# One layer of a hybrid backbone on one core: the kernel arranges every engine's instructions by its own account of durations

## The chip, the cores and the metric

The kernel runs on one core of a Trainium2 chip. The metric is device microseconds of one execution. The core has five engines that each run their own list of instructions in order: PE (matrix products), DVE and ACT (element-wise work), POOL and SP (which here mostly issue DMA transfers). "PEld" is PE's weight load, which runs beside its products. Instructions of different engines wait for each other through semaphores.

## The reference

One layer: two streams of 256 tokens (latent `x` and context `ctx`), width D = 2048, all in float32. The shift, scale and gate vectors come from two vectors `c` and `c_ctx` through one large matrix (adaLN), three mixers share one input projection, and a SwiGLU network follows.

```python
sh1_x, sc1_x, g1_x, sh2_x, sc2_x, g2_x = split(silu(c) @ w_mod + b_mod, 6)      # the same for c_ctx
hx = rmsnorm(x, norm1_g) * (1 + sc1_x) + sh1_x
hc = rmsnorm(ctx, norm1_g) * (1 + sc1_c) + sh1_c
zx, zc = hx @ w_in + b_in, hc @ w_in + b_in
s5_x = s5_mixer(zc[S5], zx[S5])            # diagonal state space, both directions, then a gated unit
ml_x = mlstm_mixer(zc[q, k, v, o, gates], zx[...])   # chunked matrix memory, both directions
cv_x = conv_module(zx[CONV])               # gated depthwise convolution and layer norm
x = x + g1_x * (concat(s5_x, cv_x, ml_x) @ w_out)
hx2 = rmsnorm(x, norm2_g) * (1 + sc2_x) + sh2_x
x = x + g2_x * ((silu(hx2 @ wg) * (hx2 @ wu)) @ w_ffn_out)
return rmsnorm(x, norm_f_g)
```

## The kernel before

**Weights.** All projection weights lie in `wst` as chunks of eight 128x128 tiles (512 KB). `raw_dma` fetches a chunk on SP's queue into `raw` (3 buffers). `split` turns it into two parts that sum to it: ACT casts `raw` to `whi` (L201, `acopy`), and DVE subtracts, `wlo = raw - whi` (L168, `tt`); 3 buffers each. The activations `hx` (latent) and `hc` (context) are held as two such parts too. `mm3` makes a product of three matmuls (whi with the high part, whi with the low part, wlo with the high part), `mm2` of two. All of these are issued by `mm` at L208 and use the whole 128x128 array at 256 or 512 columns.

**The first stage (28 to 146 us).** `main_kt` runs over 16 blocks `kt` of 128 input channels; each multiplies 7 weight tiles with the block's `hx` and `hc`, 42 matmuls, into seven accumulators (tags `ps_m`, `ps_qk`, `ps_b`). Before block `kt` can start, its `hx` and `hc` must exist, which need shift and scale of channel block `ft = kt`:

- `matvec_piece(ft, q)`, q = 0 to 3, multiplies a 512 KB piece of `w_mod` (tiles `wm`, `wmu`, `wmt`, seven buffers; DMA issued by POOL, the first ones by SP) with the vectors `cs`. It issues four matmuls at `tile_position` (0, 32 j), j = 0 to 3: each uses one strip of 32 columns of the array, with full float32 operands and 256 moving columns. These are called strips here; 16 of them make an `ft`. From `ft` = 1 on, all but the first are pinned to their place in the program (`keep_in_program_order`).
- `matvec_end(ft)`: ACT copies the result to `tmp`, PE transposes it twice (L403), DVE reduces to `as` and adds the biases.
- `make_h(ft)`: DVE normalises a block of `xr` and `cr` into `tmp`, ACT makes the high parts of `hx` and `hc` with `as` (L195), DVE the low parts.

The program writes `modulate(ft)` (the 16 strips) behind one tile of `main_kt` and `modulate2(ft)` (`matvec_end`, `make_h`) behind the next tile, some six tiles of work ahead of the block that needs them. `s5_params`, small DVE operations on 128x32 tiles (`wmt`, `s5c`, copies `LW`, `LC` at L552), is pumped in between.

**Later stages.** Up to 700 us the other tiles of the input projection and the output projection run on PE, with the S5, convolution and attention jobs as generators that `Sched` pumps between weight tiles by estimated engine time. Among their work: ACT copies `zT` to `U` (L201, x8 around 150 us) and `U` to `gT` (L201, x16 around 440 us); the gates (`rows`, transposed at L998 and L1000); and the remaining adaLN products, strips of 512 columns by groups of four. From 697 to 1448 us the SwiGLU network runs, and a final norm.

**What sets the order.** The program records instructions engine by engine; the Tile framework's scheduler then decides the order in which each engine executes them and which buffers they take, with its own estimates, except that an instruction given to `tc.keep_in_program_order` keeps its place.

Of the kernel before, what the change touches and what calls it, by code (L numbers as in the profile page):

```python
# [103 lines left out]
C_ID, C_MF, C_MR, C_K, C_SELG, NCST = 0, 128, 256, 384, 512, 640  # L104


class Sched:


    def __init__(self):  # L110
        self.pe = self.dve = self.act = 0.0
        self.jobs = []
# [34 lines left out]
            self.step(j)  # L147


@with_exitstack  # L150
def hybrid_layer_kernel(ctx: ExitStack, tc: tile.TileContext, xt, ctxt, wm1, wmr, wst, wg, bvrow, pvd, cstd, s5p, out):
    nc = tc.nc
    V, S, P, G = nc.vector, nc.scalar, nc.tensor, nc.gpsimd
# [2 lines left out]
    pre = prestack.enter_context(tc.tile_pool(name="pre", bufs=1))  # L156
    pp = ctx.enter_context(tc.tile_pool(name="pp", bufs=1, space=PSUM))
    sc = Sched()


    def n_of(ap):
        n = 1
        for s in ap.shape[1:]:
            n *= s
        return n

    def tt(o, a, b, op):
        V.tensor_tensor(out=o, in0=a, in1=b, op=op)  # L168
        sc.dve += 62 + 1.05 * n_of(o)
# [24 lines left out]
    def act(o, a, f, bias=0.0, scale=1.0, pin=False):  # L194
        i = S.activation(o, a, f, bias=bias, scale=scale)  # L195
        if pin:
            tc.keep_in_program_order(i)
        sc.act += 190 + 0.84 * n_of(o)

    def acopy(o, a):  # L200
# [3 lines left out]
    def mm(o, l, r, start, stop, native=False, tp=None, sgc=False, pin=False):  # L204
        kw = {}
        if tp is not None:
            kw["tile_position"] = tp
        i = P.matmul(o, lhsT=l, rhs=r, start=start, stop=stop, skip_group_check=sgc, **kw)  # L208
        if pin:
            tc.keep_in_program_order(i)  # L210
        n = n_of(o)
        sc.pe += (max(n * 4, 512) if native else max(n, 256)) / 2.36 / (1 if tp is None else 4)

# [12 lines left out]
    def tmp(n=512):  # L226
        return sb.tile([128, 512], F32, name="tmp", tag="tmp", bufs=4)[:, :n]
# [6 lines left out]
    cst = sb.tile([128, C_SELG], F32, name="cst")  # L234
# [22 lines left out]
    def raw_dma(c):  # L257
        raw[c] = sb.tile([128, CH * 128], F32, name="raw", tag="raw", bufs=3)
        i = nc.sync.dma_start(raw[c], wst[c])
        if phase1[0]:  # L260
            tc.keep_in_program_order(i)

    def split(c):
        his[c] = sb.tile([128, CH * 128], F32R, name="whi", tag="whi", bufs=3)
# [16 lines left out]
    def nxt(n=1):  # L281
        t = st["tile"]
        st["tile"] += n
        c, i = divmod(t, CH)
        if i == 0:
            if plan:
                plan_pump()
                fetch_to(c)
                split_to(min(c + SPL_LA, st["dma"] - 1))
            else:  # L290
                fetch_to(c + RAW_LA)
                split_to(c + SPL_LA)
        if i % PUMP_EVERY == 0:
            sc.pump()
        return his[c][:, i * 128:(i + n) * 128], los[c][:, i * 128:(i + n) * 128]

    def mm3(o, w, h, first, last, sgc=False):
        whi, wlo = w
        hhi, hlo = h
        mm(o, whi, hhi, first, False, sgc=sgc)  # L300
        mm(o, whi, hlo, False, False, sgc=sgc)
        mm(o, wlo, hhi, False, last, sgc=sgc)
# [5 lines left out]
        mm(o[:, 0:256], wlo, h[:, 0, :], False, last, sgc=True)  # L308

    def lnexp():  # L310
        tc.keep_in_program_order(S.preload_act_table_set("natural_log_exp_and_others"))

    def rsqrt(o, ps, n, scale, eps, epsv):

        y, t = tmp(n), tmp(n)
        act(y, ps, AF.Ln, bias=eps, scale=scale)
        act(y, y, AF.Exp, scale=-0.5)
        stt(t, y, -0.5 * scale, y, OP.mult, OP.mult)
        stt(t, ps, epsv / scale, t, OP.add, OP.mult)
        stt(o, t, 1.5, y, OP.add, OP.mult)  # L320
# [10 lines left out]
    def wm_dma(key, src, q=None):  # L331
        slot = (4 * key[0] + key[1]) % NWX if len(key) == 2 else 0
        if slot < NWM:
            wm[key] = sb.tile([128, 1024], F32, name="wm", tag="wm", bufs=NWM)
        else:
            wm[key] = wm_extra[slot - NWM]
        i = (q or nc.gpsimd).dma_start(wm[key], src)  # L337
        if q is not None:
            tc.keep_in_program_order(i)

    xr = pre.tile([128, KT, NT], F32, name="xr", tag="X")
    cr = sb.tile([128, KT, NT], F32, name="cr", tag="R1")
# [6 lines left out]
    def load_gates():  # L349
        wgr = tmp(256).rearrange("p (k n) -> p k n", k=KT)  # L350
        nc.sync.dma_start(wgr, wg)
        acopy(wgs[:, :, 0:16], wgr)
        tt(wgs[:, :, 16:32], wgr, wgs[:, :, 0:16], OP.subtract)
# [22 lines left out]
    cs = sb.tile([128, KT, 32], F32, name="cs")  # L376
    V.memset(cs, 0.0)
    act(cs[:, :, 0], pvc("c", 0, 16), AF.Silu)
    act(cs[:, :, 1], pvc("cc", 0, 16), AF.Silu)
    b1sc = sb.tile([128, 16], F32, name="b1sc")  # L380
# [193 lines left out]
    def main_kt(kt, hooks):  # L574
        n = 0
        for ct in range(4):
            w = nxt()
            mm3(s5b[ct][:, 256:512], w, (hx[:, kt, 0, :], hx[:, kt, 1, :]), kt == 0, kt == KT - 1, sgc=True)
            mm3(s5b[ct][:, 0:256], w, (hc[:, kt, 0, :], hc[:, kt, 1, :]), False, kt == KT - 1, sgc=True)
            hooks.get(ct, lambda: None)()  # L580
        for i in range(KHEAD):
            w = nxt()
            mm3(kb[i][:, 0:256], w, (hx[:, kt, 0, :], hx[:, kt, 1, :]), kt == 0, kt == KT - 1, sgc=True)
            mm3(kb[i][:, 256:512], w, (hc[:, kt, 0, :], hc[:, kt, 1, :]), False, kt == KT - 1, sgc=True)
            hooks.get(4 + i, lambda: None)()
# [4 lines left out]
    def modulate(ft):  # L590
        for q in range(4):
            matvec_piece(ft, q)
        plan_pump()

    def modulate2(ft):
        matvec_end(ft)
        make_h(ft)
# [7 lines left out]
    for kt in range(KT):  # L605
        hooks = {}
        for i in range(4 + KHEAD):
            t = (4 + KHEAD) * kt + i
            if t in hook_at:
                hooks[i] = lambda k=hook_at[t]: modulate(k)  # L610
            elif t - 1 in hook_at:
                hooks[i] = lambda k=hook_at[t - 1]: modulate2(k)
        main_kt(kt, hooks)
        if kt == 13:
            phase1[0] = False
            tc.keep_in_program_order(nc.sync.dma_start(cst[:, 128:], cstd[:, 128:C_SELG]))
            load_gates()
    sc.finish(pj)

# [155 lines left out]
    mj = sc.add(mod_job(), P_MOD)  # L775
# [233 lines left out]
    for ct in range(KHEAD, 8):  # L1009
        ps = mbank()  # L1010
        for kt in range(KT):
            w = nxt()
# [10 lines left out]
    for cb in range(2):  # L1023
# [3 lines left out]
        for kt in range(KT):  # L1027
            whi, wlo = nxt(4)
            for t in range(4):
                h = (hx if t < 2 else hc)[:, kt, :, 128 * (t % 2):128 * (t % 2) + 128]  # L1030
# [94 lines left out]
    q0 = st["tile"]  # L1125
# [41 lines left out]
    for ct in range(4):  # L1167
# [3 lines left out]
        sg, f = tmp(256), tmp(256)  # L1171
# [5 lines left out]
    for ct in range(KT):  # L1177
        ps = mbank()
        for i in range(8):
            src, j = (mx["c"], i) if i < 4 else (mixs, i - 4)  # L1180
# [105 lines left out]
    for kind, b in FSEQ:  # L1286
# [5 lines left out]
        last = b == NFF // FBLK - 1  # L1292
# [18 lines left out]
    i = 0  # L1311
    for n in (1, 1, 2, 2, 2, 2, 2, 2, 2):
        x = xres[:, i:i + n, :]
        tt(x, x, rs3[:, None, :].to_broadcast([128, n, NT]), OP.mult)
        nc.sync.dma_start(out[:, i:i + n, :], x)
        i += n

# [106 lines left out]
```

## Time and profile before

| | |
|---|---|
| median of 3 runs | 1461.98 us (1458.94 to 1462.68) |
| profiled execution | 1461.92 us |
| its span (first to last instruction) | 1460.2 us |
| PE busy | 1416.0 us, 97% of the span |
| PEld busy | 1242.3 us, 85% |
| DVE busy | 1058.8 us, 73% |
| ACT busy | 740.4 us, 51% |
| POOL busy | 107.3 us, 7% |
| HBM read | 311.55 MB |

A busy share is an average over stages with different limits. Rows of a timeline give start, duration, engine, line, operation, output<-inputs, count; the bracket at the end says how long the engine was idle before the row and which engine's instruction released it. Durations of single matmuls overlap (the next one enters the array while one drains), so the price of a group of matmuls is read from start to start. A full-float32 matmul that is no transpose leaves two records, so 16 strips read as x32.

### The profile page before, as it was taken

What the parts mean: (1) busy time and instruction counts of PE and PEld (TensorE: products, weight loads), DVE (VectorE), ACT (ScalarE), POOL (GpSimd) and SP (SyncE); (2) the same over time, 40 slices, a digit from 0 to 9 for tenths busy, and PEclk for the clock granted to TensorE, in tenths of its full rate; (3) what the DMA queues carried; (4) which work ended last, traced back from release to release, by engine and by line L of the source; (5) the groups of instructions that cost most, each with busy time, mean ns of one, the idle gap of its engine ahead of it and who ended that gap; (6) DMA issues with size and microseconds to landing.
All of it is one profiled execution on the core that took longest, in us unless ns stands there. A gap on an engine that the chain in (4) does not pass through costs nothing.

```text
span 1460.2 us, 25526 instructions
## 1 busy us (share of the span) xinstructions
PE 1416.0 (97%) x9856; PEld 1242.3 (85%) x9856; DVE 1058.8 (73%) x2104; ACT 740.4 (51%) x1279; POOL 107.3 (7%) x207
## 2 busy tenths in 40 slices
PE   6999899999999999999999999999999999999996
PEld 3888787887878999898998888888888888888885
DVE  7655699998988887888877778566555665556665
ACT  4334786654656555645555545433444334444353
POOL 1221111110001010011000010000000000000000
PEclk9999999999999999999999999999999999999998
DMA  9998464443436666689478787555555555555553
GB/s 365 359 359 300 156 234 142 164 165 117 143 120 226 219 238 236 243 310 343 145 234 278 277 299 240 187 189 186 189 188 187 187 188 188 188 188 188 188 177 112
DMA packets 87929, 315.31 MB, mean 216 GB/s; under 512 B 10096, under 2 KB 10880, under 8 KB 87808
## 3 DMA queue, kind: packets, MB, share of 16 engines
q1 hardware_dynamic: 60912, 216.67, 43.4%
q0 software_dynamic: 26896, 97.02, 18.8%
q8 instruction: 77, 1.26, 0.3%
q14 instruction: 44, 0.36, 0.1%
HBM read 311.55 MB, written 2.10 MB: 215 GB/s over the span
## 4 chain that ended last, share of the span: by engine, by line
PE 87%; DVE 5%; ACT 3%; DMA 2%; issue 1%; SPq 0%; DVEq 0%; ACTq 0%
PE ps_m L208 55%; PE ps_qk L208 20%; PE ps_b L208 12%; DMA raw<-in_wst_dram 1%; DVE tmp L168 1%; ACT whi L201 1%; DVE macc L179 1%; DVE wlo L168 1%; DMA tmp<-in_wg_dram 1%; ACT tmp L195 1%; PE ps_b L845 0%; ACT U L201 0%; PE ps_b L755 0%; DVE tmp L191 0%; DVE tmp L179 0%
## 5 line engine op out<-in xcount | busy, mean ns | idle before, releaser
L168 DVE TENSOR_TENSOR wlo<-raw,whi 128x1024 fp32r<-128x1024 f32 x386 | 471.3, 1222 | 268.0 <-ACT whi L201 264.4
L201 ACT CAST whi<-raw 128x1024 fp32r<-128x1024 f32 x386 | 403.8, 1047 | 478.8 <-PE ps_m L208 240.6
L208 PE MATMUL ps_m<-h,whi 128*128 128x512 f32 (+1 forms) x800 | 251.9, 369 | 3.5 <-ACT h L195 3.5
L208 PE MATMUL ps_m<-ffa,whi 128*128 128x512 f32 x704 | 248.8, 395 | 0.0
L208 PE MATMUL ps_qk<-h,whi 128*128 128x512 f32 (+1 forms) x688 | 233.2, 383 | 0.0
L208 PE MATMUL ps_m<-h,wlo 128*128 128x256 f32 x704 | 199.6, 284 | 0.0
L208 PE MATMUL ps_m<-ffa,wlo 128*128 128x256 f32 x704 | 198.9, 283 | 0.0
L208 PE MATMUL ps_m<-hx,whi 128*128 128x256 f32 x960 | 187.2, 291 | 5.5 <-ACT hx L195 3.6
L208 PE MATMUL ps_qk<-h,wlo 128*128 128x256 f32 x656 | 185.5, 283 | 0.0
L208 PEld LDWEIGHTS ps_m<-h,whi 128*128 128x128 f32 x800 | 144.9, 190 | 30.2 <-ACT h L195 4.0
L208 PEld LDWEIGHTS ps_m<-hx,whi 128*128 128x128 f32 x960 | 149.1, 190 | 24.7 <-issue 16.3
L208 PEld LDWEIGHTS ps_m<-ffa,whi 128*128 128x128 f32 x704 | 132.2, 188 | 32.2 <-issue 1.2
L208 PEld LDWEIGHTS ps_qk<-h,whi 128*128 128x128 f32 x688 | 127.2, 188 | 27.1
L179 DVE SCALAR_TENSOR_TENSOR macc<-wm,cs,macc 128x512 f32<-128x512 f32 x180 | 134.1, 745 | 6.2 <-ACT macc L195 3.8
L208 PE MATMUL ps_m<-hx,wlo 128*128 128x256 f32 x480 | 136.0, 284 | 0.0
L208 PEld LDWEIGHTS ps_m<-h,wlo 128*128 128x128 f32 x704 | 133.1, 189 | 0.0
L208 PEld LDWEIGHTS ps_m<-ffa,wlo 128*128 128x128 f32 x704 | 132.3, 188 | 0.1
L208 PEld LDWEIGHTS ps_qk<-h,wlo 128*128 128x128 f32 x656 | 123.3, 188 | 0.0
L337 POOL DMA_DIRECT2D wm<-in_wmr_dram x128 | 67.5, 528 | 607.7 <-DVE macc L179 431.3
L179 DVE SCALAR_TENSOR_TENSOR xres<-ps_m,mods,xres 128x256 f32<-128x256 f32 x160 | 76.9, 481 | 36.4 <-PE ps_m L208 34.4
L208 PEld LDWEIGHTS ps_m<-hx,wlo 128*128 128x128 f32 x480 | 91.2, 190 | 0.7 <-DVE wlo L168 0.7
L168 DVE TENSOR_TENSOR tmp<-tmp 128x256 f32<-128x256 f32 (+3 forms) x128 | 51.2, 410 | 6.1 <-ACT tmp L195 5.0
(268 smaller groups left out, 2135.7 us busy)
## 6 DMA issues: line engine op xcount, KB each, us to landing
raw<-in_wst_dram SPq DMA_DIRECT2D x386, 512.0 KB, 3.8
wm<-in_wmr_dram POOLq DMA_DIRECT2D x128, 512.0 KB, 5.3
wm<-in_wm_dram POOLq DMA_DIRECT2D x32, 512.0 KB, 7.0
wmu<-in_wm_dram POOLq DMA_DIRECT2D x16, 512.0 KB, 7.0
wmt<-in_wm_dram POOLq DMA_DIRECT2D x7, 512.0 KB, 5.8
wm<-in_wm_dram SPq DMA_DIRECT2D x5, 512.0 KB, 10.3
xr<-in_xt_dram SPq DMA_DIRECT2D x4, 512.0 KB, 6.0
cr<-in_ctxt_dram SPq DMA_DIRECT2D x4, 512.0 KB, 9.0
```

Of the source, the lines that this page charges most:

```text
L168: V.tensor_tensor(out=o, in0=a, in1=b, op=op)
L179: V.scalar_tensor_tensor(o, a, s, b, op0=op0, op1=op1)
L195: i = S.activation(o, a, f, bias=bias, scale=scale)
L201: S.copy(o, a)
L208: i = P.matmul(o, lhsT=l, rhs=r, start=start, stop=stop, skip_group_check=sgc, **kw)
L337: i = (q or nc.gpsimd).dma_start(wm[key], src)
```

## The change

The kernel no longer leaves the order to the framework. After all instructions are recorded, a new class `Arrange` reads them back, finds which ones depend on each other through the bytes they touch (`read_instructions`), gives each a duration (`account`), and places all of them by a list scheduler (`run`): at each step the engine that is free first takes, among the instructions whose inputs are ready by the account, the one that stands first in the program. Buffers of a tag go to the tiles in program order. `lay_down` then writes the order of each engine, and the turn of the buffers, as edges without semaphores, which the framework has to keep. `keep` replaces `keep_in_program_order`: a pinned instruction must follow the instruction that stands before it on its engine in the program. Arithmetic, tiles, DMAs and the number of instructions of each engine stay as they are. The tables `ranks` and `follows`, by which single instructions could be moved, are empty.

```diff
+class Arrange:
+    SEM, SAME, DMA, RATE = 45.0, 36.0, 1900.0, 345.0
...
+            if i.name in self.pins and e in last:
+                self.edge(last[e], k, 1)
...
+    def account(self, k, i, e, size):
...
+        if op == "DMACopy":
+            c = out[0][0] * out[0][3][0][1] * 4 / self.RATE
+        elif e == "PE":
+            cols = out[0][0]
+            f32r = "float32r" in str(size[0][2])
+            strip = i.tile_size[1] < 128
+            c = 6 + 0.4427 * cols if f32r else 109.0 if i.is_transpose else 2 * max(0.8438 * cols, 110.0)
+            self.mm[k] = (strip and not f32r, i.tile_position[1])
+        elif e == "DVE":
...
+            c = 150 + (2.0 if "is_tensor_tensor_scan=True" in text else 0.5 if op == "Memset" else 1.05) * n
+            c += 60 * scal
...
+        elif e == "ACT":
+            text = i.concise() if op == "Activation" else ""
+            c = 190 + 0.84 * n + 95 * scal - (40 if op == "TensorCopy" and psum else 0)
...
+    def run(self):
...
+        rank = [self.ranks.get(i.name, k) for k, i in enumerate(self.ins)]
...
+            if self.ins[k].opcode == "DMACopy":
+                clock[e] = s + (530.0 if e == "POOL" else 60.0)
+                pipe = max(s + self.DMA + (1200.0 if e == "POOL" else 0.0), pipe) + c
+                done = pipe
+            elif e == "PE":
+                strip, col = self.mm[k]
+                if strip:
+                    if strips.get("mode") != 1:
+                        s += 90
+                        strips["mode"] = 1
+                    s = max(s, strips.get(col, 0.0), strips.get("all", 0.0))
+                    strips[col] = s + c
...
+                else:
+                    s = max(s, strips.get("any", 0.0))
+                    strips["mode"] = 0
+                    clock[e] = strips["all"] = s + c
+                done = s + c + 170
...
+    def lay_down(self, engines):
+        for names in self.queue.values():
+            for s, t in zip(names, names[1:]):
...
+        for e in engines:
+            for a, b in zip(self.order[e], self.order[e][1:]):
+                self.tc.add_manual_dep(self.ins[b], self.ins[a].name, mybir.DependencyInfo(
+                    mybir.DependencyClass.NoSync, mybir.DependencyReason.DATA), reason="order")
...
+    def keep(i):
+
+        pins.add(i.ins.name)
...
-            tc.keep_in_program_order(i)
+            keep(i)
...
+    order = Arrange(tc, pins, ranks, follows)
+    order.run()
+    order.lay_down(("PE", "DVE", "ACT", "POOL", "SP"))
```

The lines of the helpers move by the new code: L208 becomes L498, L201 becomes L491, L195 becomes L485, L403 becomes L693. In the order lists below `wm`, `wmu`, `wmt` with `cs` are the strips of `matvec_piece`, the rows with `whi`, `wlo` the matmuls of `main_kt`, and `ps_b<-cst,tmp` the two transposes of `matvec_end`.

PE in the first stage, before: the strips for `ft` = 3 and, four matmul groups later, its transposes, early in block 2.

```order
71 L208 MATMUL ps_b<-wmu,cs 32x256 x4
72 L208 MATMUL ps_b<-wmt,cs 32x256 x4
73 L208 MATMUL ps_b<-wm,cs 32x256 x8
74 L208 MATMUL ps_m<-hx,whi 128x256 x2
75 L208 MATMUL ps_m<-hx,wlo 128x256
76 L208 MATMUL ps_m<-hc,whi 128x256 x2
77 L208 MATMUL ps_m<-hc,wlo 128x256
78 L403 MATMUL ps_b<-cst,tmp 128x128 x2
79 L208 MATMUL ps_m<-hx,whi 128x256 x2
80 L208 MATMUL ps_m<-hx,wlo 128x256
```

PE before, 24 rows later: the end of block 2, the strips for `ft` = 4, and the start of block 3.

```order
101 L208 MATMUL ps_b<-hc,whi 128x256 x2
102 L208 MATMUL ps_b<-hc,wlo 128x256
103 L208 MATMUL ps_b<-wm,cs 32x256 x8
104 L208 MATMUL ps_b<-wmu,cs 32x256 x8
105 L208 MATMUL ps_m<-hx,whi 128x256 x2
106 L208 MATMUL ps_m<-hx,wlo 128x256
107 L208 MATMUL ps_m<-hc,whi 128x256 x2
108 L208 MATMUL ps_m<-hc,wlo 128x256
109 L403 MATMUL ps_b<-cst,tmp 128x128 x2
```

PE with the change, at the end of block 2 and the start of block 3.

```order
102 L498 MATMUL ps_b<-hx,wlo 128x256
103 L498 MATMUL ps_b<-hc,whi 128x256 x2
104 L498 MATMUL ps_b<-wm,cs 32x256 x4
105 L498 MATMUL ps_b<-hc,wlo 128x256
106 L693 MATMUL ps_b<-cst,tmp 128x128 x2
107 L498 MATMUL ps_b<-wm,cs 32x256 x4
108 L498 MATMUL ps_m<-hx,whi 128x256
109 L498 MATMUL ps_b<-wm,cs 32x256 x4
110 L498 MATMUL ps_m<-hx,whi 128x256
111 L498 MATMUL ps_m<-hx,wlo 128x256
112 L498 MATMUL ps_m<-hc,whi 128x256 x2
113 L498 MATMUL ps_m<-hc,wlo 128x256
```

Two things moved. The 16 strips of an `ft`, which stood in one run behind the last tile of a block, now stand in pieces between matmuls of `main_kt`. And the transposes for `ft` = 3 (row 78 before, row 106 with the change), which stood almost a whole block ahead of block 3, now stand right before it, with four strips between them and the first matmul that reads what `make_h(3)` writes. In the whole order lists, the strips of 256 columns of `matvec_piece` stand in 18 runs before (14 of them of 16 strips) and in 48 with the change: 36 of 4, 9 of 8, 2 of 12 and 1 of 16. The work between the transposes of an `ft` and the first matmul that needs them is, before, 36 matmuls of `main_kt` and 16 strips for `ft` = 2 to 14. With the change it is 4 strips for `ft` = 1 and 3; 7 matmuls and 8 strips for `ft` = 2; 6 matmuls and 4 strips for `ft` = 4; 10 to 35 matmuls and up to 16 strips for the others.

ACT at the end of the first stage, before (`zT`, `kT` read the accumulators of the stage; `U` is a rearranged copy of `zT`).

```order
80 L201 CAST whi<-raw 128x1024
81 L201 COPY Wb<-tmp 64x16x16 x2
82 L195 ACTIVATE zT<-ps_m,pv 128x512
83 L195 ACTIVATE tmp<-cst,s5c 128x128
84 L195 ACTIVATE zT<-ps_m,pv 128x512 x2
85 L201 COPY Mb<-tmp 64x20x16
86 L195 ACTIVATE zT<-ps_qk,pv 128x512
87 L195 ACTIVATE kT<-ps_qk,bks 128x512
88 L201 COPY U<-zT 32x4x128
89 L195 ACTIVATE kT<-ps_b,bks 128x512 x2
90 L201 COPY U<-zT 32x4x128 x7
91 L201 CAST whi<-raw 128x1024 x2
```

ACT with the change, at the same place.

```order
75 L491 CAST whi<-raw 128x1024
76 L491 COPY bb<-bb 128x2x16
77 L485 ACTIVATE bb<-bb 128x2x16
78 L485 ACTIVATE zT<-ps_m,pv 128x512 x3
79 L491 COPY Wb<-tmp 64x16x16
80 L491 CAST wgs<-tmp 128x16x16
81 L485 ACTIVATE zT<-ps_qk,pv 128x512
82 L485 ACTIVATE kT<-ps_qk,bks 128x512
83 L485 ACTIVATE kT<-ps_b,bks 128x512 x2
84 L491 COPY U<-zT 32x4x128 x8
85 L491 CAST whi<-raw 128x1024 x3
```

The eight copies to `U` still stand ahead of the casts of the next weight chunks; ahead of them one `Wb` copy, an `Mb` copy and the `tmp` operation are gone to later places, and the cast `wgs` has come in, which stood 74th before. Around the sixteen copies to `gT` the order of ACT is, with one weight cast fewer or more beside them, the same as before, and on DVE the copies and operations on `gT` and `gs` still stand ahead of the `wlo` operations of the next chunks. From 750 us on PE's order is the same row by row, and DVE's and ACT's move by a place or two. SP's and POOL's orders are the same but for one or two places (the gate weights' DMA on SP, `bc` on POOL).

## Rows read from the trace of the kernel before

**Rows 1.** Windows: us, busy time of PE, PEld, DVE, ACT, POOL, clock, DMA share, GB/s

```profile
50.00:130.00 80.00, 80.00 (x840) 68.30 (x839) 42.28 (x111) 26.19 (x43) 21.90 (x42) 1.00 0.93 345
750.00:1448.00 698.00, 697.32 (x3983) 608.91 (x3983) 451.00 (x595) 323.45 (x471) 13.72 (x26) 1.00 0.61 204
```

**Rows 2.** PE's waits, 28 to 750 us: awaited, us in total, times, longest

```profile
PE ps_b L208 <- ACT whi L201: 4.1, 1, 4.1
PE ps_m L208 <- ACT hx L195: 3.6, 1, 3.6
PE ps_m L208 <- ACT whi L201: 1.7, 1, 1.7
PE ps_b L998 <- DVE rows L168: 1.4, 1, 1.4
PE ps_b L403 <- ACT tmp L201: 0.9, 1, 0.9
```

**Rows 3.** POOL's waits over the whole span, same columns

```profile
POOL wm L337 <- PE ps_b L208: 166.8, 24, 19.9
```

**Rows 4.** Timeline of PE, 67 to 70 us: last tile of a block, strips, next block

```profile
67.74 0.40 PE L208 MATMUL ps_b<-hc,whi 128*128 128x256 f32 x2
67.98 0.28 PE L208 MATMUL ps_b<-hc,wlo 128*128 128x256 f32 x1
68.19 0.64 PE L208 MATMUL ps_b<-wm,cs 128*32 128x256 f32 x8
68.65 1.05 PE L208 MATMUL ps_b<-wmu,cs 128*32 128x256 f32 x16
69.51 0.61 PE L208 MATMUL ps_b<-wmt,cs 128*32 128x256 f32 x8
70.05 0.50 PE L208 MATMUL ps_m<-hx,whi 128*128 128x256 f32 x2
```

**Rows 5.** Timeline of PE, 654 us: one run of four strips

```profile
654.64 0.28 PE L208 MATMUL ps_m<-mixm,wlo 128*128 128x256 f32 x1
654.85 0.64 PE L208 MATMUL ps_qk<-tmp,kc 128*32 128x256 f32 x8
655.42 0.51 PE L208 MATMUL ps_m<-mixm,whi 128*128 128x256 f32 x2
```

**Rows 6.** Timeline, 128 to 132 us: from transposes to `hx` of one `ft`

```profile
128.95 0.38 PE L403 MATMUL ps_b<-cst,tmp 128*128 128x128 f32 x2
...
130.10 0.60 ACT L195 ACTIVATE hx<-tmp,as 128x256 fp32r<-128x256 f32 x1 [1.40 <-DVE as L175]
...
130.61 0.59 ACT L195 ACTIVATE hc<-tmp,as 128x256 fp32r<-128x256 f32 x1
...
130.76 0.42 DVE L168 TENSOR_TENSOR hx<-tmp,hx 128x256 fp32r<-128x256 f32 x1
```

**Rows 7.** Timeline of DVE, 25 us: small copies in the start

```profile
25.56 0.40 DVE L552 COPY LC<-wmt 128x16 f32<-128x16 f32 x4
```

**Rows 8.** Timeline of ACT, 148 us: copies to `U`

```profile
148.98 7.81 ACT L201 COPY U<-zT 32x512 f32<-32x512 f32 x7
```

**Rows 9.** Windows behind or around three of those waits, columns as in rows 1

```profile
157.90:164.40 6.50, 6.48 (x22) 4.60 (x23) 4.00 (x4) 5.95 (x12) 0.00 (x0) 0.50 0.56 174
242.50:247.00 4.50, 3.59 (x28) 3.36 (x29) 4.34 (x9) 3.07 (x6) 0.00 (x0) 1.00 0.59 208
451.20:454.60 3.40, 3.40 (x14) 2.73 (x14) 3.40 (x4) 0.00 (x0) 0.08 (x1) 0.50 0.66 181
```

**Rows 10.** Timeline of PE, 306 to 310 us: a 512-column run, broken in two

```profile
307.03 1.04 PE L208 MATMUL ps_b<-wm,cs 128*32 128x512 f32 x2
308.01 1.10 PE L208 MATMUL ps_b<-tmp,Mb 128*128 128x64 f32 x8
...
309.71 1.06 PE L208 MATMUL ps_b<-wm,cs 128*32 128x512 f32 x6
```

**Rows 11.** Timeline of ACT, 439 us: copies to `gT`

```profile
439.37 6.88 ACT L201 COPY gT<-U 32x128 f32<-32x128 f32 x16
```

More of the change, by code (lines that the diff above doesn't have):

```diff
@@ L158, in hybrid_layer_kernel @@
     sc = Sched()
+    pins, ranks, follows = set(), {}, []
+    def keep(i):
+        pins.add(i.ins.name)
     def n_of(ap):
@@ L209, in mm @@
         if pin:
-            tc.keep_in_program_order(i)
+            keep(i)
         n = n_of(o)
@@ L260, in raw_dma @@
         if phase1[0]:
-            tc.keep_in_program_order(i)
+            keep(i)
     def split(c):
@@ L310, in lnexp @@
     def lnexp():
-        tc.keep_in_program_order(S.preload_act_table_set("natural_log_exp_and_others"))
+        keep(S.preload_act_table_set("natural_log_exp_and_others"))
     def rsqrt(o, ps, n, scale, eps, epsv):
@@ L338, in wm_dma @@
         if q is not None:
-            tc.keep_in_program_order(i)
+            keep(i)
     xr = pre.tile([128, KT, NT], F32, name="xr", tag="X")
@@ L615, in hybrid_layer_kernel @@
             phase1[0] = False
-            tc.keep_in_program_order(nc.sync.dma_start(cst[:, 128:], cstd[:, 128:C_SELG]))
+            keep(nc.sync.dma_start(cst[:, 128:], cstd[:, 128:C_SELG]))
             load_gates()
```

221 lines of the change are left out of this document (added).

## The prediction

> **What bounds the kernel now.** I read the windows first, then PE's waits, then the timelines of the places that the new order touches. From 750 us on PE is busy for 697.32 of 698 us, and between 50 and 130 us for 80.00 of 80, both at the full granted clock of 2.4 GHz [rows 1]. So in these two stretches any time that PE loses or saves is time of the kernel. The second thing to see is what PE waits for between 28 and 750 us [rows 2]. No row of that view names a DMA; the waits are for casts of weights on ACT (4.1 and 1.7 us), for the first `hx` (3.6), for the gates' `rows` (1.4) and for one `tmp` copy (0.9). The transfers of the adaLN pieces in turn wait for PE: POOL's queue stood 166.8 us for a buffer that PE had still to read [rows 3]. So the first stage goes at PE's pace, and what the order of PE costs there is paid in full.
>
> About 0.3% (4.4 us) is what a measurement of this kernel can tell from no change.
>
> **The change, part by part.** Nothing is computed more or less. The order lists show which places moved. From 750 us on PE's order is unchanged and PE never waits, so I count that stretch at nothing: DVE is busy 451.00 of its 698 us and ACT 323.45 [rows 1], which covers moves of a place or two on either. If that cover were gone, a late `wlo` would stop PE for at most the shift, about one operation.
>
> *Broken runs of strips, +6.8 us.* A run of strips has a price of its own beside its work. In one run of 16, the last whole-array matmul starts at 67.98 and the next one at 70.05, so 2.07 us; two whole-array matmuls take 0.24 from start to start (67.74 to 67.98), one 0.12, so the run costs 1.95 [rows 4]. A run of four: 654.64 to 655.42 is 0.78, less 0.12 is 0.66 [rows 5]. Twelve more strips cost 1.29, so four cost 0.43, and 0.23 of each run is the change of the array from whole to strips and back. The lists hold 48 such runs instead of 18. Thirty more at 0.227 (the rows before rounding) are 6.8 us, all in a stretch where PE has no free time. The kernel's own account charges 0.09 for a change, by which it would be 2.7; that is the lower bound, the measured rows decide for 6.8. A few of the new pieces stand before 35 us, where PE is still slow, so up to 8 is possible.
>
> *Transposes close to their use, +3.0 us.* From the transposes at 128.95 to the end of the high part of `hx` (130.10 + 0.60) is 1.75 us; the low part is done at 131.18, 2.23 behind the transposes [rows 6]. Before, 36 matmuls and 16 strips lie between (36 x 0.12 + 1.95 = 6.3 us), so nobody waits. With the change four strips (0.66) lie between for `ft` = 1 and 3: a wait of 1.1 us each; the second matmul comes behind another four strips, which cover the low part. For `ft` = 4 there are 6 matmuls and 4 strips, 0.72 + 0.66 = 1.38: 0.4 for the high part, and 0.3 more for the low one. For `ft` = 2, 0.84 + 1.09 in one run of eight or two of four: at most 0.1. The other eleven have 2.3 us or more. Together 3.0. At best none of it is new, where another wait comes first; at worst 4, where DVE is late with the reduction, since a `wlo` stands just ahead of it for `ft` = 4.
>
> Whether such a wait also costs clock is read from its neighbours. After the 1.7 us wait the granted clock was 0.50 (1.2 GHz) from 451.2 to 454.6; after the 4.1 us wait, from 157.9 to 164.4; around the 1.4 us wait it stayed 1.00 [rows 2, 9]. The new waits of 1.1 lie nearest to the 1.4, so I take no drop. The Trainium skill, page "TensorE: Matmul & The Clock Gate", section on HAM oscillation, describes a kernel in which waits for data put PE back to its lower clock tile after tile, each next tile starting cold. If that held for `ft` = 1, 3 and 4, the stretches behind them would run at half speed for a while, which is the third rival below.
>
> *The start, -0.4.* DVE's small copies `LC` and `LW` of `s5_params`, which stood between the operations that lead to the first `hx`, go behind them; PE waits for that `hx` [rows 2]. One row of them takes 0.40 [rows 7]. Other small operations come in their place, so the gain is between 0 and 1.
>
> *The cast of the gate weights, -0.9.* PE's last transposes wait 0.9 for a `tmp` copy [rows 2], which stood behind the cast `wgs` on ACT, and that cast waits for its DMA. The cast now comes some places later, when the data has long arrived. Between 0 and 0.9.
>
> *Broken runs made whole, -2.0.* Two runs of four strips with 512 columns stood as 1 + 3. Strips of one run work side by side, so the single one cost as much as a whole run: 307.03 to 308.01, 0.98 [rows 10]. Both are whole now. Between 0 and 2.0.
>
> *The gates' transposes, -1.2.* PE's transposes of `rows` stand some ten matmuls later, about 1.2 us, in front of a wait of 1.4 [rows 2]. At the same time DVE does other work ahead of the next `rows`. Between +1 and -1.4.
>
> *The copies to `U`, -0.5.* Seven of eight take 7.81 us on ACT [rows 8], and the cast that PE waits 4.1 us for is behind them. The order keeps that. Ahead of them `Wb`, `Mb` and a `tmp` operation have gone, and `wgs` has come. I take half a microsecond; the half clock stays. Between +1 and -2. The same for the sixteen copies to `gT`, 6.88 us [rows 11], in front of the 1.7 us wait: they keep their place, and I take 0, between +3 and -3.4.
>
> The sum is 6.8 + 3.0 - 0.4 - 0.9 - 2.0 - 1.2 - 0.5 = +4.8. The profiled execution took 1461.92 us (span 1460.2 and 1.7 around it), 0.06 under the median of the runs; so 1466.7 us. What the change gains lies in waits that are small, because the two long waits are kept by ACT operations that the account prices too low: it gives a copy to `U` 190 + 0.84 x 512 = 620 ns, where the row shows 7.81 / 7 = 1.12 us.
>
> **The rivals.**
>
> *A: the transfers set the pace of the first stage (faster).* If the DMA, not PE, decided when a block can go on, more runs of strips would fill time that PE spends waiting anyway, as the kernel's account believes (it reckons 345 GB/s). Then the 6.8 and the 3.0 vanish and -5.0 is left: 1456.9. For it: a DMA share of 0.93 at 345 GB/s [rows 1]. Against it: PE idles for nothing there, and POOL waits for PE [rows 1, 3]. It decides if PE in the present order would fall behind the transfers by less than the 9.8 us that the new order adds. Chance 0.17.
>
> *B: the long waits shrink enough (no change).* The wait of 4.1 us and the half clock behind it cost 4.1 + 6.5 / 2 = 7.3; those at 450 us 1.7 + 3.4 / 2 = 3.4 [rows 2, 9]. If the run of copies to `U` starts 2.7 us earlier, the wait falls to the 1.4 that did no harm, and 2.7 + 3.2 = 5.9 come back, 5.4 more than counted: 1461.3. With the other place too, 1457.9. For it: three ACT operations have gone from ahead of the copies. Against it: all eight copies still are there, and each takes over a microsecond. Chance 0.18.
>
> *C: the new waits take the clock down (slower by more).* If the waits before blocks 1, 3 and 4 are followed by 1.2 GHz as the 1.7 us wait was, each costs another 1.7 (half of 3.4) to 3.2 [rows 9]. Three times 2.2 is 6.5: 1473.2. It decides between waits of 1.4 and 1.7 us; mine are 1.1. Chance 0.13.
>
> **How the numbers follow.** The forecast has 0.52, A 0.17, B 0.18, C 0.13. The forecast's own spread, a few microseconds, lies on both sides of +4.4: 0.29 above, 0.21 between, 0.02 below -4.4. A gives 0.12 faster and 0.05 no change, B 0.06 and 0.12, C all slower. So faster 0.20, same 0.38, slower 0.42. The range runs from A's 1456 to C's 1474, which leaves out the cases where several bounds meet on one side; the forecast alone lies between 1461 and 1471.
>
> **What would show it.** In the profile after, a block of the first stage lasts 0.5 us longer (two more runs), and the stretch from the first `hx` to the last tile of block 15 some 9 us. PE's waits name ACT `hx` or DVE `hx` again, three to four times for about 1 us, all before 70 us. The waits for `whi` at 158 and 450 us stand there nearly unchanged with the half clock behind them, the wait for `tmp` before the last transposes is gone, and from 750 us on everything has the same length. I am wrong if the first stage is not longer (A), if the half clock near 158 us is missing (B), or if new stretches of 1.2 GHz appear in the first 70 us (C).

## The result and the profile after

| | before | after |
|---|---|---|
| median | 1461.23 us (4 runs, 1458.94 to 1462.68) | 1469.47 us (4 runs, 1467.0 to 1470.08) |
| ratio | | 1.0055, 95% interval 1.0036 to 1.0073 |
| profiled execution, its span | 1461.92, 1460.2 us | 1470.08, 1468.3 us |

The change makes the kernel 0.55% slower, 8.2 us. The forecast was 1466.7 us, 4.8 slower. The windows of the profile after answer to [rows 1]: between 50 and 130 us PE is no longer busy all the time, and from 750 us on it still is.

```profile
50.00:130.00 80.00, 78.81 (x735) 59.45 (x735) 36.77 (x96) 22.87 (x38) 20.01 (x39) 1.00 0.87 305
750.00:1448.00 698.00, 698.00 (x4005) 610.59 (x4004) 458.29 (x603) 332.56 (x480) 14.77 (x28) 1.00 0.60 206
```

The count of PE records in the first row fell from 840 to 735: in the same 80 us less of the program is done. Some of PE's waits between 28 and 750 us, in the columns of [rows 2]:

```profile
PE ps_m L498 <- DVE wlo L458: 4.2, 5, 1.6
PE ps_b L498 <- ACT whi L491: 3.9, 1, 3.9
PE ps_m L498 <- ACT hx L485: 0.9, 2, 0.5
PE ps_m L498 <- DVE vx L458: 0.8, 1, 0.8
PE ps_b L498 <- DVE as L477: 0.7, 2, 0.3
PE ps_b L693 <- ACT tmp L491: 0.2, 1, 0.2
```

The wait for `whi` at 158 us stands there as before, 3.9 for 4.1 us. The wait of 1.7 for `whi` at 450 us, that of 1.4 for `rows` and that of 0.9 for the `tmp` copy are gone. New are waits for `vx`, `hx` and, in front of strips, for the reduction `as`; for `wlo` there are five instead of one of 0.6 us. Two of the new ones stand where the wait at 450 us was, so that place has not become free of waits:

```profile
453.74 0.48 PE L498 MATMUL ps_m<-hx,whi 128*128 128x256 f32 x2 [0.77 <-DVE vx L458]
458.89 0.39 PE L498 MATMUL ps_m<-hx,wlo 128*128 128x256 f32 x1 [1.60 <-DVE wlo L458]
```

The view also has rows that neither [rows 2] nor the prediction names. The wait of 3.5 us for the first `h` of the SwiGLU network is the same in both kernels; one for `RH` near 590 us has shrunk (first row before, second row after):

```profile
PE ps_m L208 <- ACT RH L195: 1.2, 1, 1.2
PE ps_m L498 <- ACT RH L485: 0.3, 1, 0.3
```

**Where the time went.** I compare the start of the same instruction in both traces. The first matmul of `main_kt` starts at 27.97 us before and 26.52 after, 1.45 earlier. The last one of block 15 starts at 146.69 before and 158.19 after, 11.5 later. From there to the end of the span it is 1313.5 us before and 1310.1 after. So the first stage lost 13.0 us behind its first matmul, 1.45 were won ahead of it, and 3.4 are won back later.

Inside the first stage, PE's timeline shows one piece of strips that stands between two tiles:

```profile
62.79 0.40 PE L498 MATMUL ps_qk<-hc,whi 128*128 128x256 f32 x2
63.03 0.28 PE L498 MATMUL ps_qk<-hc,wlo 128*128 128x256 f32 x1
63.24 0.64 PE L498 MATMUL ps_b<-wmu,cs 128*32 128x256 f32 x8
63.81 0.50 PE L498 MATMUL ps_b<-hx,whi 128*128 128x256 f32 x2
64.15 0.28 PE L498 MATMUL ps_b<-hx,wlo 128*128 128x256 f32 x1
```

As in [rows 5] the run costs 63.81 - 63.03 - 0.12 = 0.66 up to the next matmul. But the row behind it shows more: its two matmuls take 0.34 from start to start (63.81 to 64.15), where the two of the first row take 0.24. So a run has a tail of 0.10 in the second matmul behind it, which I had not counted. Where only one matmul stands between two runs, the second run itself comes that much later, and the matmul behind it 0.76 instead of 0.66. Blocks 5 to 8, with two runs more each and no wait, last 7.93 to 7.95 us for 7.26 before, 0.34 for each run.

The transposes of `ft` = 3 and the start of block 3, whose order is shown ahead of the prediction:

```profile
56.09 0.44 PE L693 MATMUL ps_b<-cst,tmp 128*128 128x128 f32 x2 [0.18 <-ACT tmp L491]
56.87 0.64 PE L498 MATMUL ps_b<-wm,cs 128*32 128x256 f32 x8 [0.34 <-DVE as L477]
57.96 0.39 PE L498 MATMUL ps_m<-hx,whi 128*128 128x256 f32 x1 [0.45 <-ACT hx L485]
```

The transposes wait 0.18 for ACT's copy, the strips behind them 0.34 for DVE's reduction `as`, and the first matmul of block 3 waits 0.45 for `hx`: 0.97 in all, in two more steps than forecast but of the forecast size (1.1). For `ft` = 1 it is 0.79. Before block 4 no wait is listed as idle time, but the starts lie further apart:

```profile
65.66 0.64 PE L498 MATMUL ps_b<-wmt,cs 128*32 128x256 f32 x8
66.43 0.86 PE L498 MATMUL ps_m<-hx,whi 128*128 128x256 f32 x2
67.13 0.28 PE L498 MATMUL ps_m<-hx,wlo 128*128 128x256 f32 x1
67.25 0.53 PE L498 MATMUL ps_m<-hc,whi 128*128 128x256 f32 x2
67.61 0.28 PE L498 MATMUL ps_m<-hc,wlo 128*128 128x256 f32 x1
```

From the strips to the next matmul it is 0.77 instead of 0.57, the first pair takes 0.70 instead of 0.34, the second 0.36 instead of 0.24: about 0.7 in all. Before block 2 it is 0.1.

The granted clock, in the columns of [rows 9]:

```profile
24.20:34.40 10.20, 7.33 (x39) 4.33 (x40) 8.82 (x57) 3.09 (x4) 1.58 (x3) 0.50 1.03 408
167.60:174.30 6.70, 5.03 (x21) 3.15 (x22) 3.50 (x3) 6.60 (x14) 1.05 (x2) 0.50 0.37 116
345.10:348.40 3.30, 3.30 (x9) 2.52 (x9) 3.26 (x6) 0.00 (x0) 0.00 (x0) 0.50 0.66 210
```

At the start PE falls to 1.2 GHz at 24.2 us already; before, that was at 27.9, and in both kernels the full clock comes back between 34 and 35 us. Since the first matmul now starts at 26.52, 7.9 us of PE's work run at half speed instead of 6.8, which takes back some 0.5 of the 1.45. The spell behind the wait for the `whi` at 158 us (now at 169) is as long as before. The one at 451 us is gone: behind the waits of 0.77 and 1.60 us that stand there now the granted clock stays at 1.00. A new one stands at 345 us, behind two short waits:

```profile
343.27 0.62 PE L498 MATMUL ps_b<-XB,kc 128*32 128x256 f32 x2 [0.83 <-DVE XB L469]
344.81 0.63 PE L498 MATMUL ps_m<-wlo,hx 128*128 128x512 f32 x1 [0.91 <-DVE wlo L458]
```

### The profile page after: what moved, and what is told of

It is laid out like the page before. It is cut to its first block, busy times and chain, and to the rows that moved or that the text cites. A ratio compares the mean times of both kernels' runs of the same rounds, so it can differ in the third digit from the quotient of the medians.

```text
span 1468.3 us, 25563 instructions
## 1 busy us (share of the span) xinstructions
PE 1422.9 (97%) x9856; PEld 1239.8 (84%) x9856; DVE 1062.1 (72%) x2104; ACT 745.1 (51%) x1279; POOL 107.5 (7%) x207
## 4 chain that ended last, share of the span: by engine, by line
PE 85%; DVE 7%; ACT 3%; DMA 2%; issue 2%; POOL 0%; DVEq 0%; ACTq 0%; POOLq 0%
PE ps_m L498 52%; PE ps_qk L498 20%; PE ps_b L498 12%; DMA raw<-in_wst_dram 2%; DVE wlo L458 1%; DVE tmp L458 1%; DVE macc L469 1%; ACT whi L491 1%; DVE XB L469 1%; PE ps_b L1045 0%; DMA wm<-in_wmr_dram 0%; DVE tmp L469 0%; PE ps_b L1135 0%; ACT U L491 0%; DVE Vr L458 0%
## 5 line engine op out<-in xcount | busy, mean ns | idle before, releaser
L491 ACT CAST whi<-raw 128x1024 fp32r<-128x1024 f32 x386 | 404.1, 1048 | 419.5 <-PE ps_m L498 274.7
L498 PE MATMUL ps_m<-h,whi 128*128 128x512 f32 (+1 forms) x800 | 252.4, 369 | 3.5 <-ACT h L485 3.5
L498 PE MATMUL ps_m<-ffa,whi 128*128 128x512 f32 x704 | 248.2, 395 | 0.0
L498 PE MATMUL ps_qk<-h,whi 128*128 128x512 f32 (+1 forms) x688 | 233.1, 383 | 0.0
L498 PE MATMUL ps_m<-h,wlo 128*128 128x256 f32 x704 | 199.7, 284 | 0.0
L498 PE MATMUL ps_m<-ffa,wlo 128*128 128x256 f32 x704 | 198.4, 282 | 0.0
L498 PE MATMUL ps_m<-hx,whi 128*128 128x256 f32 x960 | 188.1, 290 | 5.7 <-ACT hx L485 4.7
L498 PE MATMUL ps_qk<-h,wlo 128*128 128x256 f32 x656 | 185.6, 283 | 0.0
L498 PEld LDWEIGHTS ps_m<-hx,whi 128*128 128x128 f32 x960 | 149.0, 189 | 28.7 <-issue 15.5
L498 PEld LDWEIGHTS ps_m<-h,whi 128*128 128x128 f32 x800 | 145.1, 190 | 30.4 <-ACT h L485 4.0
L498 PEld LDWEIGHTS ps_m<-ffa,whi 128*128 128x128 f32 x704 | 132.3, 188 | 31.8 <-issue 1.2
L498 PEld LDWEIGHTS ps_qk<-h,whi 128*128 128x128 f32 x688 | 127.3, 188 | 27.1
L498 PE MATMUL ps_m<-hx,wlo 128*128 128x256 f32 x480 | 136.8, 286 | 2.4 <-DVE wlo L458 2.4
L498 PEld LDWEIGHTS ps_m<-h,wlo 128*128 128x128 f32 x704 | 133.2, 189 | 0.0
L498 PEld LDWEIGHTS ps_m<-ffa,wlo 128*128 128x128 f32 x704 | 132.2, 188 | 0.1
L498 PEld LDWEIGHTS ps_qk<-h,wlo 128*128 128x128 f32 x656 | 123.5, 188 | 0.0
L498 PEld LDWEIGHTS ps_m<-hx,wlo 128*128 128x128 f32 x480 | 90.6, 189 | 8.0 <-issue 4.1
```

The costliest lines, as they stand in the source:

```text
L491: S.copy(o, a)
```

## The experiments

Each kernel was compared with the kernel before on the same chip; ratios are to it. "First stage" below is how much later than before the last matmul of block 15 starts, in the profiled execution (after: +11.5 us).

**Whole runs, transposes left late.** An edge in the account from the last piece of an `ft` to its first strip.

```diff
+        landed[key] = i.ins.name            # in wm_dma
...
+            if (q, j) == (0, 0):            # in matvec_piece
+                opens[ft] = i.ins.name
...
+    for ft in range(1, KT):
+        order.edge(order.index[landed[ft, 3]], order.index[opens[ft]])
```

> The change with one kind of edge more: the first strip of each ft from 1 on must wait, in the kernel's own account, for the last of the four pieces of w_mod, so that the 16 strips stand in one run again (15 runs of 16 in the order, instead of 36 of 4 and 9 of 8). The transposes stay late: 6, 0, 1 and 14 matmuls before the first use for ft 1 to 4. Theory (the price of a run, 0.227 us, is the main loss): 6.8 us and about 1 us for split pairs come back, the waits for hx at blocks 1 to 4 grow from 3.0 to about 5.5 us; 1464 to 1465. Rival 1 (the runs cost nothing, the late transposes cost all): 1471 to 1473. Rival 2 (waits of about 2 us now take the clock down in the first 70 us): 1468 to 1472, with 1.2 GHz in stretches that the change has not.

Measured: 1470.66 us, 1.0078 (1.0064 to 1.0092); first stage +8.55. So by the total it is no gain, and by the total alone the late transposes would seem to decide everything. The trace says otherwise. The runs are whole and blocks 5 and 6 last 7.26 us again (blocks 7 to 11, with only 13 to 17 matmuls between the transposes and their use, 0.2 to 0.6 more), but PE now waits longer for `hx` before blocks 2 and 3, and both waits are followed by half clock:

```profile
47.22 0.85 PE L499 MATMUL ps_m<-hx,whi 128*128 128x256 f32 x2 [1.42 <-ACT hx L486]
```

```profile
58.06 0.86 PE L499 MATMUL ps_m<-hx,whi 128*128 128x256 f32 x2 [1.30 <-ACT hx L486]
```

```profile
49.20:52.50 3.30, 3.30 (x18) 3.30 (x17) 1.90 (x3) 1.05 (x1) 0.00 (x0) 0.50 0.60 243
59.40:62.70 3.30, 3.30 (x17) 3.25 (x16) 0.00 (x0) 0.74 (x1) 0.00 (x0) 0.50 0.66 262
390.50:397.20 6.70, 5.94 (x21) 5.03 (x21) 6.06 (x15) 5.39 (x15) 0.00 (x0) 0.50 0.02 2
```

Each of the two spells costs 1.7 us (half of 3.4). That is what the third rival of the prediction described, seen at waits of 1.42 and 1.30 us. The third spell follows another wait that this order makes later (next experiment), worth 7 us. What the first stage won is lost there.

**PE's first stage in program order.**

```diff
+    pe = [k for k, e in enumerate(order.eng) if e == "PE"][70:973]
+    for a, b in zip(pe, pe[1:]):
+        order.edge(a, b, 1)
```

> The change, with the PE instructions of the first stage (all but the first 70 of 973) held in program order by edges; the list scheduler arranges everything else around them. Runs are whole and the transposes stand 36 matmuls and 16 strips ahead of their use, as before. Theory (the whole loss is PE's order in the first stage, and the later stages of the change gain 3 us): the 11.5 us that the first stage became longer come back, 1456 to 1459, under the kernel before. Rival (the order of DVE and ACT costs as much): 1463 to 1468.

Measured: 1460.55 us, 1.0012 (1.0003 to 1.0021); first stage -1.2, that is 12.7 us better than the change. Nearly every block again lasts 7.26 us, and at 370 us the kernel is 5.4 us ahead of before. There this order makes PE wait for the S5 job, with half clock around it:

```profile
380.29 1.94 PE L498 MATMUL ps_b<-tmp,Mb 128*128 128x64 f32 x8 [4.10 <-DVE tmp L458]
```

```profile
378.80:385.50 6.70, 5.21 (x20) 4.75 (x21) 6.06 (x17) 4.96 (x14) 0.00 (x0) 0.50 0.00 0
```

The clock falls at 378.8, while PE still waits, so 5.3 us of work behind the wait run at half speed. 4.1 and half of 5.3 are 6.8; behind it the kernel is 1.4 us late. So the first stage is settled, the total missed by that wait (1456 to 1459 was expected).

**Only PE laid down; all but PE laid down.**

```diff
-    order.lay_down(("PE", "DVE", "ACT", "POOL", "SP"))
+    order.lay_down(("PE",))                            # one kernel
+    order.lay_down(("DVE", "ACT", "POOL", "SP"))       # the other
```

> The change, but only PE's order is laid down as edges (and the turn of the buffers); DVE, ACT, POOL and SP are ordered by the framework around it. Theory (PE's order is the cause): 1467 to 1471, with the first stage as long as in the change. Rival (the order of DVE and ACT is the cause): 1459 to 1463.

Measured: 1481.31 us, 1.0149 (1.0135 to 1.0163); first stage +14.5. Its first matmul starts at 30.28, 2.3 us later than before; from there to the last one of block 15 it is 130.9 us, in the change 131.7, before 118.7. So the first stage is as long as in the change. The whole is worse than the change itself: with PE held to an order and the other engines ordered by other rules, they miss each other, most of all at 712 us, where PE waits 6.9 us for the first `h` of the SwiGLU network (3.5 in the change). The expectation was too low, but the direction is that of the theory.

> The change, but the order is laid down for DVE, ACT, POOL and SP only; the framework orders PE, which gives runs of 16 strips in the first stage and the transposes 7 to 36 matmuls and 16 strips ahead of their use. Theory (PE's order is the cause): 1458 to 1463. Rival (the order of DVE and ACT is the cause): 1467 to 1471.

Measured: 1461.69 us, 1.0016 (1.0007 to 1.0024); first stage +0.8. As expected from PE's order as the cause: with the change's orders of DVE, ACT, POOL and SP, and PE left to the framework, nearly 6 of the change's 8 us are gone (by the ratios).

**The price of a run by itself.** The kernel before, its four pieces written behind four successive tiles.

```diff
-            if t in hook_at:
-                hooks[i] = lambda k=hook_at[t]: modulate(k)
-            elif t - 1 in hook_at:
-                hooks[i] = lambda k=hook_at[t - 1]: modulate2(k)
+            for q in range(4):
+                if t - q in hook_at:
+                    hooks[i] = lambda k=hook_at[t - q], q=q: (matvec_piece(k, q), plan_pump() if q == 3 else None)
+            if t - 4 in hook_at:
+                hooks[i] = lambda k=hook_at[t - 4]: modulate2(k)
```

> The kernel before, ordered by the framework as before, but with the 16 strips of each ft written as four pieces behind four successive weight tiles (and the transposes one tile behind the last piece). The order holds 62 runs of strips, 60 of them of 4, instead of 18; the transposes still stand 11 to 18 matmuls and 4 strips ahead of their use, so hx is ready. It measures the price of a run by itself. Theory (0.227 us for each of 44 more runs): 10 us more than the kernel before, 1468 to 1471, all of it in the first stage, and no wait for hx. Rival (runs are hidden behind the transfers): within 2 us of the kernel before.

Measured: 1475.04 us, 1.0109 (1.0095 to 1.0123); first stage +13.9, by 1.01 in nearly every block, with a single wait for `hx` of 0.2 us. That is more than the 1468 to 1471 that was expected, since a run costs more than I had taken. So the runs do cost, nothing of them is hidden behind transfers, and three more in a block cost 0.34 each, where I had 0.227:

```profile
72.79 0.28 PE L208 MATMUL ps_b<-hc,wlo 128*128 128x256 f32 x1
73.00 0.64 PE L208 MATMUL ps_b<-wm,cs 128*32 128x256 f32 x8
73.57 0.50 PE L208 MATMUL ps_m<-hx,whi 128*128 128x256 f32 x2
73.91 0.28 PE L208 MATMUL ps_m<-hx,wlo 128*128 128x256 f32 x1
```

Again 0.66 up to the next matmul (72.79 to 73.57, less 0.12), and 0.34 instead of 0.24 behind it.

**The account's transfer rate.** Why does the account split the strips? By its 345 GB/s a piece lands too late for its place, and PE takes the next matmul that is ready. The trace gives 366 GB/s between 28 and 50 us.

```diff
-    SEM, SAME, DMA, RATE = 45.0, 36.0, 1900.0, 345.0
+    SEM, SAME, DMA, RATE = 45.0, 36.0, 1900.0, 366.0    # one kernel
+    SEM, SAME, DMA, RATE = 45.0, 36.0, 1900.0, 400.0    # the other
```

> The change with one number of its account changed: the transfer rate is 366 GB/s, as the trace shows between 28 and 50 us, instead of 345. The order then holds 37 runs instead of 48, and only the transposes of ft 3 stand right before their use. Theory (the account believes that the transfers pace the first stage, and splits the strips for that): 2.5 us from runs, about 1 from split pairs and 2 to 3 from waits come back: 1462 to 1465. Rival (the late transposes alone decide, see the run with whole runs): 1465 to 1467 only if the waits were worth all of it. If the rate does not matter: 1469.

Measured: 1462.06 us, 1.0019 (1.0008 to 1.0031); first stage +5.4, no wait for `hx` behind the first.

> The same with 400 GB/s, more than the chip gives, so that the account never sees PE wait for a transfer in the first stage. 24 runs, 20 matmuls or more between transposes and use. Theory: 5.5 us from runs, 1 from pairs, 3 from waits: 1459 to 1462. Rival (an account that is wrong about the transfers places strips before their data is there, and PE waits for DMA): 1464 or more, with waits for DMA in the first stage.

Measured: 1458.05 us, 0.9991 (0.9982 to 1.0000); first stage -0.85, and in the first stage, behind its start, PE waits for no DMA. So one number of the account, 6% under what the trace shows, is worth 5 to 9 us by the ratios: the splitting comes from it. The rate that is 9% too high does better than the right one, so it is not that the account became truer; at 400 it sees no wait of PE for transfers in the first stage, and leaves most runs whole (24 instead of 48).

**A better arrangement.** First with PE's first stage in program order, 366 GB/s, 0.227 instead of 0.09 us for a change to strips, and the casts ranked early.

```diff
+    for k, i in enumerate(order.ins):
...
+        if order.eng[k] == "ACT" and to is not None and "whi" in to:
+            ranks[i.name] = k - 100
```

> The change with four things: PE's first stage in program order, 366 GB/s, 0.227 us for a change of the array to strips, and the casts of weights on ACT ranked 100 places earlier than they stand in the program, so that they go ahead of jobs such as the copies to U. By the account no wait of PE over 1.3 us is left between 40 and 560 us. Theory (with the first stage whole, the later stages are worth what PE waits there and at 1.2 GHz): 1449 to 1456, under both kernels. Rival (what the account cannot see comes back as new waits, as the 4.1 us wait at 380 us of the run with PE's program order): 1458 to 1464.

Measured: 1457.42 us, 0.9986 (0.9977 to 0.9994). At 430 us it was 7.2 us ahead of before, then PE waited 3.8 us for `vx`, which DVE computes behind the sixteen copies to `gT`. There the account falls behind the trace: it spaces the copies by 0.20 us on DVE, the trace shows 0.29. Two more kernels put these prices right, with ranks and without.

```diff
+    early = {("ACT", "whi"): 150, ("DVE", "vx"): 60, ("DVE", "wlo"): 40}      # empty in the second
+    dear = {("ACT", "U"): 1210.0, ("ACT", "gT"): 525.0, ("DVE", "gT"): 370.0}
...
+        if to in dear and names[-1] in ("zT", "U"):
+            order.cost[k] = dear[to]
+        if to in early:
+            ranks[i.name] = k - early[to]
```

> As the run with the first stage in program order and casts ranked earlier, with the account's prices of the copies to U (ACT 1.21 us) and gT (ACT 0.525, DVE 0.37) put right after the trace, and with ranks by which whi goes 150 places, vx 60 and wlo 40 places ahead of the program. By the account no wait of PE over 1.26 us is left between 40 and 660 us, and the end is 7.4 us ahead of that of the next kernel. Theory (in the later stages PE waits for casts and for vx because jobs stand ahead of them, and each wait over some 1.5 us is followed by 1.2 GHz): no half clock between 40 and 690 us, 1449 to 1455. Rival (the account misses as much as it finds): 1456 to 1462 with other waits.

Measured: 1448.50 us, 0.9926 (0.9913 to 0.9939), 11 us under the kernel before, the best of all. PE's longest waits between 28 and 750 us, and that for `whi`:

```profile
PE ps_m L498 <- ACT h L485: 3.6, 1, 3.6
PE ps_b L498 <- DVE XB L469: 2.2, 1, 2.2
PE ps_m L498 <- ACT tmp L485: 2.0, 1, 2.0
PE ps_b L498 <- ACT Mb L491: 1.2, 2, 0.9
PE ps_m L498 <- ACT whi L491: 0.6, 1, 0.6
```

The waits for `whi` at 158 and at 450 us are gone (the one of 0.6 stands at 593). Two short spells of half clock are left between 40 and 690 us (3.4 us each, at 167 and at 580, around the waits of 2.2 for `XB` and 2.0 for `tmp`), where I had expected none.

> The same without the ranks: PE's first stage in program order, 366 GB/s, 0.227 us for a change to strips, and the right prices of the copies to U and gT. Theory (better prices alone do not help, since the scheduler goes by the place in the program and knows nothing of what is urgent): waits of 2 us and more near 190 and 380 us, and 1457 to 1462, about as the run with PE's program order alone. Rival (the wrong prices were the cause of the later waits): 1449 to 1455.

Measured: 1456.54 us, 0.9977 (0.9968 to 0.9987); waits of 2.48 us for `whi` at 157 us and 1.91 for the S5 job at 379, each with half clock, and one of 1.99 for `wlo` at 193 without. As expected, right prices alone leave the waits; the ranks are worth the 8.0 us between the two kernels, where the account had said 7.4.

## Why the prediction was right or wrong

The direction, the place and the cause were right; the size was too small by 3.4 us. Step by step:

| step | forecast | measured |
|---|---|---|
| 30 more runs of strips | +6.8 (0.227 each) | +10.2 (0.34 each) |
| transposes close to their use | +3.0 | +2.6 (0.79, 0.97, about 0.7 before block 4, 0.1 before block 2) |
| the start | -0.4 | -1.45, of which 0.5 is lost at 1.2 GHz |
| cast of the gate weights | -0.9 | -1.1 (block 14: 6.43 to 5.30 us) |
| first stage | +8.5 | +11.5 |
| later stages | -3.7 | -3.4 |

The measured parts of the first stage add up to 10.8 of the 11.5. 0.4 more is a wait for `wlo` at 28.12 us (0.55, where before 0.17 was waited for `hx`); the rest is open.

**Broken runs.** This is the mis-sized term. I measured a run from the last matmul ahead of it to the first one behind it, and stopped one instruction too early: the second matmul behind it comes 0.10 late as well. [rows 5] would have shown it one row further on. With 0.34 the sum is +8.2, and the forecast 1470. That it then meets the measured 8.2 to the tenth is luck, since parts of the other terms were off both ways. The other bounds of this term, nothing (hidden behind transfers, the first rival) and 0.09 (the account's), are excluded by the split version of the kernel before.

**Late transposes.** Right in size and in place. That the waits do not take the clock down held for the first stage of the change: behind its start no 1.2 GHz appears in the first 70 us, so the third rival did not come. But the reason that I gave, the length of the wait, does not hold. Before, a wait of 1.4 us left the clock at 1.00 [rows 2, 9]; with whole runs, waits of 1.42 and 1.30 were followed by 0.50. In the change, the waits of 0.83 and 0.91 at 343 and 345 us were followed by 0.50, and that of 1.60 at 459 us was not. In the last kernel of the experiments, 1.91 us was and 1.99 was not, and with PE left to the framework a wait of 2.39 us for `vx` at 446 us was not either. So the line between 1.4 and 1.7 us, on which the prediction and an expectation rested, is none, and that the waits of 1.1 left the clock alone was not to be known from it. What decides was not tried. The Trainium skill, page "TensorE: Matmul & The Clock Gate", describes in its section on HAM oscillation a kernel in which waits for data put PE back to the lower clock, tile after tile. With whole runs the trace shows that behind two waits in a row (1.42 and 1.30 us, granted clock 0.50), in the first stage of the change not.

**The start.** The gain was larger than forecast, but most of it does not come from the small copies. 0.65 of the 1.45 us is there already at PE's first matmul (8.72 us before, 8.07 after), ahead of all of them: before, ACT's first operation on `xr` waited 0.61 for its DMA, in the change it did not. The split kernel, which the framework orders as before, has this matmul at 8.36, so a part is no gain of the order at all. Where the copies stood, from DVE's operation at 23.18 to the one on `xr` and `rst` at 25.87, 2.69 us became 2.40: 0.3, close to the forecast 0.4. The rest lies in between and was not taken apart. PE's fall to the lower clock came earlier with it and took a part back.

**The later stages.** The sum was close, its parts were not, and that it was close is luck. The gates' transposes gave their wait back (PE's lag falls by 2.3 us between 240 and 250 us, 1.2 forecast), and the runs made whole show as about 1 us each, as forecast. At 450 us, which I had put at 0, a wait of 1.7 and its half clock went, 3.4 us, but 0.77 and 1.60 are now waited there, so some 1.0 is left. The shorter wait for `RH` gave 0.9, for which the sum had no term. Against that stand a wait of 0.92 for an S5 job at 208 us, a longer spell of half clock around the first `h` (703.4 to 710.2 us, before 696.9 to 700.4; some 0.6), and the waits at 343 and 345 us and their half clock, 3.4 us, none of which I saw. PE arrives at 343 us earlier relative to DVE than before (PE is 7.0 us behind its old time, DVE 8.2), so most of what PE had won since 158 us was waited for again. The second rival, the long waits shrinking, is refuted at 158 us (3.9 for 4.1) and came true in part at 450 us.

**From 750 us on** nothing was forecast, and PE's order is as before. A wait of 0.22 for `wlo` at 750.13 us is gone; behind it this stretch is 0.9 us shorter in the profiled execution. 0.8 of that lies in one place, the products into `ps_m` from `ffa` that start at 1133.76 us before: 352 records take 62.18 us before and 61.40 after, in both without a wait and at the full clock. The kernels with whole runs, with PE in program order, with only PE laid down, with split runs and with 366 GB/s take 62.2 there too, the other five 61.4. So it does not go with the order of the first stage; what sets it is open.

The forecast of +4.8 lay only 0.4 us above the 4.4 that it counted as no change, because of the term for the runs; with it right, slower would have had most of the chance.

## What to carry to other kernels

A list scheduler with fixed prices is only as good as the price that decides at the bottleneck: here a transfer rate 6% too low made it fill PE's supposed waiting time with pieces whose change of array mode it hardly charged. A rate that was 9% too high did better still, since more of the pieces then stayed together. Before laying an order down, compare the account's start times with a trace at a few places, and price a group of instructions from the last normal step ahead of it to the first normal step behind it. An order in program order with right prices still lacks urgency: ranking what the bottleneck engine waits for (casts, `vx`, `wlo`) ahead of jobs gave 8.0 us, where the right prices, with PE's first stage in program order, had given 5 over that order alone, by the ratios.

## What the runs showed of the hardware

A run of four full-float32 matmuls on 32-column strips between whole-array matmuls costs 0.34 us beside its work, alike in the kernel before, in the change and in the split version: 0.66 to the next matmul and 0.10 in the one behind that, less 0.43 for the strips themselves. How long PE waited did not tell whether 1.2 GHz followed: behind waits of 1.30, 1.42, 1.71 and 1.91 us the granted clock was 0.50, behind others of 1.44, 1.60, 1.99 and 2.39 us it stayed at 1.00. And the lag of 11.5 us that PE brought out of the first stage did not vanish in the next one: at 335 us PE was still 7.0 us behind its old time, and DVE, which was busy 173 of the 194 us between 146 and 340 us, was 8.2 behind.
